# Conditioning sums of gate 0 and layer 1 moved behind layer 0's attention, in pages of their own, half of them on ScalarE and GpSimd

## The chip, the cores and the metric

The kernel runs on one core of one Trainium2 chip. Its time is the device time of one execution in microseconds (us): 2407.33 is the median of three runs (2405.7 to 2408.84). A core has a matrix engine (TensorE, PE in the profile, with its weight loads as PEld), three engines for elementwise work (VectorE or DVE, ScalarE or ACT, GpSimd or POOL) and a queue engine (SyncE or SP) that here issues the large loads. Each works through its own list of instructions in order, and semaphores tie them together. Tiles lie in SBUF, 128 partitions wide; TensorE writes to PSUM, which has 8 banks of 128x512 fp32.

## The reference, cut to what matters

Two transformer blocks on 256 latent tokens and 256 context tokens of width 2048, batch 1. The first block has two layers whose norm and residual are conditioned: a vector `c` (latent) and a vector `c_ctx` (context) each go through a 2048 x 6144 matrix per layer, and the 6144 sums are shift, scale and gate.

```python
for l in range(2):
    last = l == 1
    shift, scale, gate = split(silu(c) @ ada_w[l] + ada_b[l], 3)             # latent
    shift_c, scale_c, gate_c = split(silu(c_ctx) @ ada_w[l] + ada_b[l], 3)   # context
    h  = rmsnorm(x,  norm_g[l]) * (1 + scale)   + shift
    hc = rmsnorm(xc, norm_g[l]) * (1 + scale_c) + shift_c
    # q, k, v, pool, fourier, gate inputs: h @ w_in[l]; the context in layer 1 gives only k and v
    att = attention(q, [kc; k], [vc; v])                # 8 heads of 128, 2 kv heads
    mixed = concat(att, multiscale_pool(up), fourier_mix(uf))
    x = x + gate * ((mixed * silu(g)) @ w_out[l])
    if not last:                                        # the same for the context
        xc = xc + gate_c * outc
# then a second block: w_in (4096 columns), gating, a recurrent scan, w_out, a gated FFN of width 6144
```

`ada_w` is 2 x 2048 x 6144 fp32, 100.7 MB, read once. Layer 1 needs the context's shift and scale but not its gate.

## The kernel before, in words

**Weights.** Every projection is a list of steps. A step asks for one tile of 128x1024 fp32 of a weight (512 KB, `wraw`, a ring of 4), splits it into a rounded part `whi` (a cast on ScalarE, L259) and a remainder `wlo` (a subtraction on VectorE, L260), and multiplies three products per pair (`mm3`, L203 to L205): 24 matmuls of 512 columns, or 24 of 256 where only one half of the tokens is multiplied. `execute` (L111) walks the list: it issues the loads of coming steps on SP in the order of the list (`_issue`, L101), at least 3 ahead, and splits up to 3 weights ahead, with high priority.

**Conditioning.** Layer 0's shift and scale are multiplied on TensorE in the startup, from pages of 128x512 (`apage`, in ring B). All others are summed on VectorE: `ada_span` (L306) covers 512 columns; it loads 8 tiles of two 128x512 blocks into the same `wraw` ring as the weights, and for each of the 16 blocks does one multiply-add by a per-partition column of silu(c) for the latent (accumulator in SBUF, ring E of 2) and, if `nm` is 2, one for the context (accumulator in the PSUM bank `ada`): L322 for the first block, L324 for the others. ScalarE then copies the accumulators to S tiles (L329), and `ada_sum` adds over the partitions with ones on TensorE (L341), transposes (L348) and adds the bias (L355).

**Order.** After the startup, layer 0's list `main` runs: the last quarter of the k, v, q, Fourier and pool projections (9 steps), 32 attention tasks queued, the constants of block 2 queued, pool channels (4 steps), gate groups 2, 3, 0, 1 (8 steps each; all tasks are flushed ahead of group 0, which needs attention's output), and the output projection `w_out`, three groups over both token halves and one group for each half (8 steps each). 14 spans (four of layer 0's gate, eight of layer 1's shift and scale, two of layer 1's gate for the latent alone) make 112 steps, dealt out evenly over the list from its start to 12 steps ahead of its end. The last two spans lie in layer 1's list, from its entry 20 at 0.6 a step.

**Tasks.** The tails (q and k norms, attention heads, pool, Fourier, `ada_sum`) are generators in a queue; `tick` starts up to one per two slots of 1.25 us of TensorE work, four at a time. A planner orders each engine's instructions by priority, which follows the order of the list, and by what it expects to be ready.

**Rings.** B has 12 tiles of 128x512: in the attention of layer 0 they are kT (2), v (2) and qT (8). S (9 tiles) serves short-lived results. Layer 1 uses B for k, q and pool tiles too.

Of the kernel before, what the change touches and what calls it, by code (L numbers as in the profile page):

```python
# [8 lines left out]
F32 = mybir.dt.float32  # L9
F32R = mybir.dt.float32r  # L10
AF = mybir.ActivationFunctionType
ALU = mybir.AluOpType
# [20 lines left out]
class Kern:  # L33
# [22 lines left out]
    def S(self, name, dt=F32, shape=(P, 512)):  # L56
        return self.pg.tile(list(shape), dt, tag="S", bufs=9, name=name)

# [32 lines left out]
    def _issue(self, kind, src, nk, width):  # L91

        if kind == "page":
            raw = self.B("apage")
        else:
            raw = self.pg.tile([P, 1024], F32, tag="wraw", bufs=4, name="wraw")
        dst = raw[:, :width]
        if nk > 1:
            dst = dst.rearrange("p (k c) -> p k c", k=nk)
            src = src.rearrange("(k p) c -> p k c", p=P)  # L100
        self.nc.sync.dma_start(dst, src)  # L101
        return raw
# [8 lines left out]
    def execute(self, steps, ahead=3):  # L111
# [3 lines left out]
        for reqs, fn in steps:  # L115
            n = len(reqs)
            if not n:
                fn()
                continue
            while len(ready) < min(len(plan), p + n + max(ahead, 2 * n)):  # L120
                ready.append(self._issue(*plan[len(ready)]))
# [183 lines left out]

    def ada_span(self, l, c0, nm):  # L306

        w = self.a["ada_w"]
        acc = []

        def step(k0, wt):
            nc = self.nc
            if k0 == 0:
                acc.append(self.E("acc0"))
                if nm == 2:
                    acc.append(self.bank("ada", "acc1"))
            for k in (k0, k0 + 1):
                x = wt[:, (k - k0) * 512:(k - k0 + 1) * 512]
                for m in range(nm):
                    cm = self.silu_c[:, m * 16 + k:m * 16 + k + 1]  # L320
                    if k == 0:
                        nc.vector.tensor_scalar(acc[m], x, cm, None, ALU.mult)  # L322
                    else:
                        nc.vector.scalar_tensor_tensor(acc[m], x, cm, acc[m], ALU.mult, ALU.add)  # L324
            if k0 == KT - 2:
                sums = []
                for m in range(nm):
                    sums.append(self.S("ada_acc"))
                    nc.scalar.copy(sums[m], acc[m])  # L329
                self.defer(self.ada_sum, l, c0, sums)  # L330
        return [([("raw", w[l, k * P:(k + 2) * P, c0:c0 + 512], 2, 1024)],
                 partial(step, k)) for k in range(0, KT, 2)]

# [179 lines left out]
    def bcast_cols(self, col, nt):  # L513
        nc = self.nc
        r = self.misc("rbc")
        for t in range(nt):
            b = self.small("bcw", (P, P))
            if t % 2:
# [156 lines left out]
    def attention(self, g, t, h):  # L675
# [13 lines left out]
        nc.vector.reciprocal(rc, sm)  # L689
        nc.vector.tensor_scalar(p[:, :nk], p[:, :nk], rc, None, ALU.mult)  # L690
        yield 3
# [81 lines left out]
    def layer0(self):  # L773
# [13 lines left out]
        fm = lambda c0, n, evac, **kw: self.proj_fm(w_in, c0, n, ks, hi, lo, NT, evac, **kw)  # L787
        pool = lambda b: (lambda t, ps: self.pool_branch(b + t, ps, NT))
        p01 = fm(1536, 256, pool(0), tags=["misc", "misc"])

# [7 lines left out]
        def part(i):  # L798
            ks = list(range(4 * i, 4 * i + 4))
            st = self.proj_tm(w_in, 1024, 512, ks, hi, lo, 4, lambda t, h, ps: self.part_kv(i, t, ps))  # L800
            for g in range(2):
                st += self.proj_tm(w_in, g * 512, 512, ks, hi, lo, 4, lambda t, h, ps, g=g: self.part_q(i, g, t, ps))
            return st + self.proj_fm(w_in, 2048, 512, ks, hi, lo, NT, partial(self.part_fourier, i)) + [p01[i]]
        parts = [part(i) for i in range(4)]
# [12 lines left out]
        for l, first, last in ((0, 4096, 6144), (1, 0, 4096)):  # L817
            for c0 in range(first, last, 512):
                ada += self.ada_span(l, c0, 2)
        for c0 in range(4096, 5120, 512):  # L820
            ada += self.ada_span(1, c0, 1)
        later = lambda fn, *args: ([], partial(self.defer, fn, *args))
        flush = [([], self.flush)]
        main = [later(self.mix_consts, 0)] + parts[3]
        main += [later(self.attention, g, t, h) for g in range(2) for t in range(4) for h in range(4)]
        main.append(([], self.setup_late))
# [8 lines left out]
        for g in (2, 3, 0, 1):  # L835
            if g == 0:
                main += flush
            elif g == 2:
                main.append(([], lambda: self.until(lambda: self.npf == 8)))
# [36 lines left out]
        for m in (1, 0):  # L876
# [3 lines left out]
            main.append(later(self.h_layer1, m))  # L880
        n_proj = sum(1 for st in main if st[0]) - 12
        out, acc, done = [], 0.0, 0
        for st in main:
            out.append(st)
# [44 lines left out]
    def layer1(self):  # L929
# [35 lines left out]
        ada = []  # L965
        for c0 in range(5120, 6144, 512):
            ada += self.ada_span(1, c0, 1)
        main, ada = self.mix_in(main, ada, first=20, per=0.6)
        steps += main + ada
# [59 lines left out]
    def block2_consts(self):  # L1029
# [3 lines left out]
        lam = self.col("lru_lambda", 0, 8)  # L1033
        T = lambda n: self.one("spl_" + n, [P, 8])
        u, z, z2, s, m = T("u"), T("z"), T("z2"), T("s"), T("m")
        nc.scalar.activation(u, lam, AF.Abs)
# [398 lines left out]
```

## Time and profile before

| | |
|---|---|
| median of three runs | 2407.33 us |
| the profiled execution | 2400.92 us |
| its span, first to last instruction | 2398.9 us |
| PE busy | 2284.9 us (95%) |
| DVE busy | 1628.3 us (68%) |
| ACT busy | 1008.9 us (42%) |
| POOL busy | 208.7 us (9%) |
| conditioning sums on DVE (L324) | 302.5 us, 420 instructions |
| PE's granted clock, mean | 0.981 |

Times are microseconds unless marked ns. A busy PE is not a PE at its peak: matmuls are pipelined and their ends are modelled, so a matmul that waits for its weights can look long. The clock is the mean of TensorE's two levels, 1.2 and 2.4 GHz, as a share of the higher. A row of a group of instructions gives the line, the engine, the operation, what it writes and reads with shapes, the count, busy time and mean, then the engine's idle time just before them and what ended most of it. A row of waits names who waited for whom. An fp32 matmul that is not in the rounded form leaves two records.

### The profile page before, as it was taken

The page shows a single profiled execution, that of the slowest core. Times are in us where ns is not written, and L with a number is a line of the kernel's source. Part 1 is how long each engine was busy: PE and PEld are TensorE (multiplying, and loading weights), DVE is VectorE, ACT ScalarE, POOL GpSimd, SP SyncE. Part 2 cuts the span into 40 slices and gives each one's busy share as a digit, 9 for nine tenths or more (in the row PEclk, how much of TensorE's full clock was granted, in tenths as well). Part 3 has the DMA queues.
Part 4 walks back from the last instruction along what each step waited for, and adds up shares of the span by engine and source line. Part 5 has one row for each costly group of instructions (what it writes and reads, how often), then busy time and mean ns, then how long its engine had stood idle before and what let it go on. Part 6 is the DMA issues. An engine that isn't in the chain of part 4 may idle for free. (4 is left out here: it accounts for less than half of the span.)

```text
span 2398.9 us, 37437 instructions
## 1 busy us (share of the span) xinstructions
PE 2284.9 (95%) x14672; PEld 1991.8 (83%) x14672; DVE 1628.3 (68%) x2603; ACT 1008.9 (42%) x1507; POOL 208.7 (9%) x262
## 2 busy tenths in 40 slices
PE   7999789999798999999999999999999999999998
PEld 3777567877576887889998799999999999988886
DVE  3345987889888786755577966667667666664444
ACT  3321323422322364434454744445445545543433
POOL 1000221010101111010032211110000000000100
PEclk9999889999999999999999999999999999999999
DMA  9866442456766755755554455556666656665554
GB/s 316 277 231 188 135 145 82 136 161 202 233 214 190 256 173 176 221 157 159 182 178 158 141 187 167 193 183 185 185 185 183 184 183 183 215 210 187 186 190 151
DMA packets 202721, 447.89 MB, mean 187 GB/s; under 512 B 15848, under 2 KB 60288, under 8 KB 202544
## 3 DMA queue, kind: packets, MB, share of 16 engines
q1 hardware_dynamic: 193088, 428.93, 57.3%
q0 software_dynamic: 3888, 11.18, 1.4%
q10 hardware_dynamic: 5568, 5.40, 0.7%
q8 instruction: 115, 1.88, 0.3%
q14 instruction: 62, 0.51, 0.1%
HBM read 437.05 MB, written 8.39 MB: 186 GB/s over the span
## 5 line engine op out<-in xcount | busy, mean ns | idle before, releaser
L260 DVE TENSOR_TENSOR wlo<-wraw,whi 128x1024 fp32r<-128x1024 f32 x608 | 749.0, 1236 | 532.8 <-ACT whi L259 529.7
L259 ACT CAST whi<-wraw 128x1024 fp32r<-128x1024 f32 x608 | 635.9, 1049 | 980.8 <-PE acc L204 448.3
L203 PE MATMUL acc<-phi,whi 128*128 128x256 f32 (+1 forms) x1600 | 483.7, 302 | 17.6 <-ACT whi L259 16.4
L205 PE MATMUL acc<-phi,wlo 128*128 128x256 f32 (+1 forms) x1600 | 474.7, 299 | 4.9 <-DVE wlo L260 4.7
L204 PE MATMUL acc<-plo,whi 128*128 128x256 f32 (+1 forms) x1600 | 478.7, 299 | 0.0
L203 PE MATMUL acc<-h3t,whi 128*128 128x256 f32 x1536 | 434.3, 283 | 1.3 <-DVE xT L1257 1.3
L205 PE MATMUL acc<-h3t,wlo 128*128 128x256 f32 x1536 | 433.9, 283 | 0.0
L204 PE MATMUL acc<-h3t,whi 128*128 128x256 f32 x1536 | 433.9, 283 | 0.0
L203 PEld LDWEIGHTS acc<-phi,whi 128*128 128x128 f32 x1600 | 306.2, 191 | 35.2 <-ACT whi L259 21.0
L205 PEld LDWEIGHTS acc<-phi,wlo 128*128 128x128 f32 x1600 | 305.7, 191 | 18.1 <-DVE wlo L260 8.3
L324 DVE SCALAR_TENSOR_TENSOR acc<-wraw,silu_c,acc 128x512 f32<-128x512 f32 x420 | 302.5, 760 | 17.3 <-DMA wraw<-in_ada_w_dram 16.3
L204 PEld LDWEIGHTS acc<-plo,whi 128*128 128x128 f32 x1600 | 306.2, 191 | 9.5 <-issue 0.9
L203 PEld LDWEIGHTS acc<-h3t,whi 128*128 128x128 f32 x1536 | 293.3, 191 | 1.7 <-DVE xT L1257 1.7
L205 PEld LDWEIGHTS acc<-h3t,wlo 128*128 128x128 f32 x1536 | 293.4, 191 | 0.2
L204 PEld LDWEIGHTS acc<-h3t,whi 128*128 128x128 f32 x1536 | 293.4, 191 | 0.0
L203 PE MATMUL acc<-hhi,whi 128*128 128x512 f32 x384 | 167.2, 435 | 10.5 <-ACT whi L259 10.5
L204 PE MATMUL acc<-hlo,whi 128*128 128x512 f32 x384 | 154.7, 403 | 0.0
L204 PE MATMUL acc<-wlo,act 128*128 128x512 f32 x384 | 151.7, 395 | 0.0
L203 PE MATMUL acc<-whi,act 128*128 128x512 f32 x384 | 151.7, 395 | 0.0
L205 PE MATMUL acc<-whi,act 128*128 128x512 f32 x384 | 151.7, 395 | 0.0
L205 PE MATMUL acc<-hhi,wlo 128*128 128x512 f32 x384 | 148.7, 401 | 0.8 <-DVE wlo L260 0.8
L203 PEld LDWEIGHTS acc<-hhi,whi 128*128 128x128 f32 x384 | 73.7, 192 | 36.8 <-ACT whi L259 16.8
(354 smaller groups left out, 2828.1 us busy)
## 6 DMA issues: line engine op xcount, KB each, us to landing
wraw<-in_w_in_dram SPq DMA_DIRECT2D x216, 512.0 KB, 4.2
wraw<-in_ffn_w_up_dram SPq DMA_DIRECT2D x192, 512.0 KB, 3.6
wraw<-in_ada_w_dram SPq DMA_DIRECT2D x128, 512.0 KB, 4.2
wraw<-in_w_out_dram SPq DMA_DIRECT2D x104, 512.0 KB, 4.6
wraw<-in_ffn_w_down_dram SPq DMA_DIRECT2D x96, 512.0 KB, 4.6
apage<-in_ada_w_dram SPq DMA_DIRECT2D x128, 256.0 KB, 5.6
xd<-xT SPq DMA_DIRECT2D x16, 256.0 KB, 3.0
xT<-xd POOLq DMA_DIRECT2D x16, 256.0 KB, 4.6
```

What stands on the lines that cost most here:

```text
L203: mm(out, lhi, rhi, start=start, stop=False)
L204: mm(out, lhi, rlo, start=False, stop=False)
L205: mm(out, llo, rhi, start=False, stop=stop)
L259: self.nc.scalar.copy(hi, src)
L260: self.nc.vector.tensor_tensor(lo, src, f(hi), ALU.subtract)
L324: nc.vector.scalar_tensor_tensor(acc[m], x, cm, acc[m], ALU.mult, ALU.add)
```

## The change

The list of spans is now 12 of two vectors each in layer 0 (four of layer 0's gate, eight of layer 1's shift and scale), dealt out from the end of gate group 2 (`first`) to 10 steps ahead of the end of `main`; layer 1's own four gate spans, for the latent alone, all lie in layer 1's list, from its entry 18 at 1.6 a step. A span's loads are 16 pages of 128x512 (256 KB) from ring B, one step each. The latent's accumulator moves to the PSUM bank and the context's to an E tile. In every span but each fourth (`pool`), the context's half is done by a scaling in place on ScalarE, after VectorE has read the page, and an add on GpSimd into the E tile. Loads now run ahead until two weights beyond the present step are asked for. Weights have 5 tiles, S has 8; the small tiles of the block 2 constants and of the broadcasts move into S. Attention's tasks are queued after each group of q rather than after all parts, and the division by the softmax sum goes from VectorE to ScalarE.

```diff
...
@@ -93,7 +93,7 @@
         if kind == "page":
             raw = self.B("apage")
         else:
-            raw = self.pg.tile([P, 1024], F32, tag="wraw", bufs=4, name="wraw")
+            raw = self.pg.tile([P, 1024], F32, tag="wraw", bufs=5, name="wraw")
         dst = raw[:, :width]
         if nk > 1:
             dst = dst.rearrange("p (k c) -> p k c", k=nk)
@@ -117,7 +117,8 @@
             if not n:
                 fn()
                 continue
-            while len(ready) < min(len(plan), p + n + max(ahead, 2 * n)):
+            while len(ready) < len(plan) and (len(ready) < p + n + max(ahead, 2 * n) or sum(
+                    r[0] == "w" for r in plan[p + n:len(ready)]) < 2):
                 ready.append(self._issue(*plan[len(ready)]))
             while nsplit < len(ready) and (plan[nsplit][0] != "w" or live < 3):
                 if plan[nsplit][0] == "w":
@@ -303,33 +304,34 @@
         ins = nc.vector.scalar_tensor_tensor(self.gs[l][:, t0:t0 + nb, :], ad[:, s, :], 1.0, gain, ALU.add, ALU.mult)
         self.fin = getattr(ins, "ins", ins).name
 
-    def ada_span(self, l, c0, nm):
+    def ada_span(self, l, c0, nm, pool=False):
 
         w = self.a["ada_w"]
         acc = []
 
-        def step(k0, wt):
+        def step(k, x):
             nc = self.nc
-            if k0 == 0:
-                acc.append(self.E("acc0"))
+            if k == 0:
+                acc.append(self.bank("ada", "acc0") if nm == 2 else self.E("acc0"))
                 if nm == 2:
-                    acc.append(self.bank("ada", "acc1"))
-            for k in (k0, k0 + 1):
-                x = wt[:, (k - k0) * 512:(k - k0 + 1) * 512]
-                for m in range(nm):
-                    cm = self.silu_c[:, m * 16 + k:m * 16 + k + 1]
-                    if k == 0:
-                        nc.vector.tensor_scalar(acc[m], x, cm, None, ALU.mult)
-                    else:
-                        nc.vector.scalar_tensor_tensor(acc[m], x, cm, acc[m], ALU.mult, ALU.add)
-            if k0 == KT - 2:
+                    acc.append(self.E("acc1"))
+            for m in range(nm):
+                cm = self.silu_c[:, m * 16 + k:m * 16 + k + 1]
+                if m and pool:
+                    nc.scalar.activation(x if k else acc[m], x, AF.Copy, scale=cm)
+                    if k:
+                        nc.gpsimd.tensor_tensor(acc[m], acc[m], x, ALU.add)
+                elif k == 0:
+                    nc.vector.tensor_scalar(acc[m], x, cm, None, ALU.mult)
+                else:
+                    nc.vector.scalar_tensor_tensor(acc[m], x, cm, acc[m], ALU.mult, ALU.add)
+            if k == KT - 1:
                 sums = []
                 for m in range(nm):
                     sums.append(self.S("ada_acc"))
                     nc.scalar.copy(sums[m], acc[m])
                 self.defer(self.ada_sum, l, c0, sums)
-        return [([("raw", w[l, k * P:(k + 2) * P, c0:c0 + 512], 2, 1024)],
-                 partial(step, k)) for k in range(0, KT, 2)]
+        return [([("page", w[l, k * P:(k + 1) * P, c0:c0 + 512], 1, 512)], partial(step, k)) for k in range(KT)]
 
     def ada_sum(self, l, c0, sums):
         nc = self.nc
...
@@ -687,7 +689,7 @@
         nc.scalar.activation(p[:, :nk], sc[:, :nk], AF.Exp, bias=mx, accum_out=sm)
         rc = self.small("rc", (P, 1))
         nc.vector.reciprocal(rc, sm)
-        nc.vector.tensor_scalar(p[:, :nk], p[:, :nk], rc, None, ALU.mult)
+        nc.scalar.activation(p[:, :nk], p[:, :nk], AF.Copy, scale=rc)
         yield 3
         tp = self.misc("pTp")
         for c in range(nk // P):
...
@@ -800,6 +803,8 @@
             st = self.proj_tm(w_in, 1024, 512, ks, hi, lo, 4, lambda t, h, ps: self.part_kv(i, t, ps))
             for g in range(2):
                 st += self.proj_tm(w_in, g * 512, 512, ks, hi, lo, 4, lambda t, h, ps, g=g: self.part_q(i, g, t, ps))
+                if i == 3:
+                    st += [later(self.attention, g, t, h) for t in range(4) for h in range(4)]
             return st + self.proj_fm(w_in, 2048, 512, ks, hi, lo, NT, partial(self.part_fourier, i)) + [p01[i]]
         parts = [part(i) for i in range(4)]
         steps = ada_chunk(0, 256)
@@ -816,13 +821,9 @@
         ada = []
         for l, first, last in ((0, 4096, 6144), (1, 0, 4096)):
             for c0 in range(first, last, 512):
-                ada += self.ada_span(l, c0, 2)
-        for c0 in range(4096, 5120, 512):
-            ada += self.ada_span(1, c0, 1)
-        later = lambda fn, *args: ([], partial(self.defer, fn, *args))
+                ada += self.ada_span(l, c0, 2, pool=len(ada) // KT % 4 != 3)
         flush = [([], self.flush)]
         main = [later(self.mix_consts, 0)] + parts[3]
-        main += [later(self.attention, g, t, h) for g in range(2) for t in range(4) for h in range(4)]
         main.append(([], self.setup_late))
         main += fm(2048 - 256, 256, pool(2))
         order = list(range(8, 16)) + list(range(8))
@@ -835,6 +836,8 @@
         for g in (2, 3, 0, 1):
             if g == 0:
                 main += flush
+            elif g == 3:
+                first = len(main)
             elif g == 2:
                 main.append(([], lambda: self.until(lambda: self.npf == 8)))
             gate = fm(2560 + g * 512, 512, lambda t, ps, g=g: self.gate(g * 4 + t, ps, NT))
@@ -878,9 +881,9 @@
             main += self.proj_fm(w_out, 1536, 512, order, lambda k, s=s: self.pr[k][0][:, s],
                                  lambda k, s=s: self.pr[k][1][:, s], NX, partial(evac_half, m))
             main.append(later(self.h_layer1, m))
-        n_proj = sum(1 for st in main if st[0]) - 12
-        out, acc, done = [], 0.0, 0
-        for st in main:
+        n_proj = sum(1 for st in main[first:] if st[0]) - 10
+        out, acc, done = main[:first], 0.0, 0
+        for st in main[first:]:
             out.append(st)
             if st[0]:
                 acc += len(ada) / n_proj
@@ -963,9 +966,9 @@
                 main.append(([], self.flush))
             main += self.proj_fm(w_in, 2560 + g * 1024, 1024, ks, hi, lo, NX, partial(evac_g, g))
         ada = []
-        for c0 in range(5120, 6144, 512):
+        for c0 in range(4096, 6144, 512):
             ada += self.ada_span(1, c0, 1)
-        main, ada = self.mix_in(main, ada, first=20, per=0.6)
+        main, ada = self.mix_in(main, ada, first=18, per=1.6)
         steps += main + ada
         order = list(range(8, 16)) + list(range(8))
 
...
```

## Rows read from the trace of the kernel before

**Rows 1.** Busy us (xcount) of PE, PEld, DVE, ACT, POOL by stretch; clock, DMA, GB/s.

```profile
233.00:469.00 236.00, 208.05 (x950) 161.57 (x949) 201.10 (x397) 75.97 (x153) 36.17 (x56) 0.93 0.42 128
469.00:872.00 403.00, 371.21 (x1822) 292.87 (x1821) 340.89 (x565) 127.14 (x195) 43.49 (x52) 0.97 0.65 204
872.00:1060.00 188.00, 175.49 (x1017) 146.02 (x1015) 135.32 (x246) 90.52 (x157) 19.87 (x32) 0.98 0.61 185
1640.00:1660.00 20.00, 20.00 (x171) 20.00 (x170) 8.74 (x8) 7.30 (x8) 0.00 (x0) 1.00 0.62 184
2200.00:2220.00 20.00, 20.00 (x88) 16.05 (x86) 8.57 (x7) 7.74 (x8) 0.00 (x0) 1.00 0.60 188
```

**Rows 2.** Groups of TensorE's instructions, 233 to 469 us: busy us, mean ns, idle before.

```profile
L700 PE MATMUL pv<-pT,v 128*128 128x128 f32 x142 | 19.3, 276 | 0.0
...
L682 PE MATMUL sc<-kT,qT 128*128 128x512 f32 x32 | 16.1, 593 | 0.0
...
L752 PE MATMUL fz<-ab,mix 128*128 128x256 f32 x32 | 9.7, 447 | 3.0 <-DVE mix L618 3.0
```

**Rows 3.** Timeline of TensorE about 402 us: start us, us from first to last end.

```profile
401.83 0.59 PE L682 MATMUL sc<-kT,qT 128*128 128x256 f32 x2
402.27 1.16 PE L700 MATMUL pv<-pT,v 128*128 128x128 f32 x8
403.27 1.04 PE L694 MATMUL pTp<-ident,p 128*128 128x128 f32 x8
404.06 0.48 PE L204 MATMUL acc<-hlo,whi 128*128 128x512 f32 x1
```

**Rows 4.** Groups of TensorE's instructions, 469 to 872 us.

```profile
L203 PE MATMUL acc<-phi,whi 128*128 128x512 f32 x192 | 80.7, 421 | 16.1 <-ACT whi L259 15.9
...
L203 PE MATMUL acc<-phi,whi 128*128 128x256 f32 x128 | 37.3, 291 | 0.5 <-ACT whi L259 0.2 <-DVE xT L855 0.2
```

**Rows 5.** Groups of TensorE's instructions, 872 to 1060 us.

```profile
L203 PE MATMUL acc<-whi,phi 128*128 128x512 f32 x115 | 47.9, 416 | 0.0
...
L203 PE MATMUL acc<-phi,whi 128*128 128x256 f32 x137 | 40.8, 298 | 0.3 <-ACT whi L259 0.3
```

**Rows 6.** Groups of VectorE's instructions, 233 to 469 us.

```profile
L324 DVE SCALAR_TENSOR_TENSOR acc<-wraw,silu_c,acc 128x512 f32<-128x512 f32 x127 | 91.9, 763 | 0.8 <-DMA wraw<-in_ada_w_dram 0.6
```

**Rows 7.** Groups of VectorE's instructions, 469 to 872 us.

```profile
L324 DVE SCALAR_TENSOR_TENSOR acc<-wraw,silu_c,acc 128x512 f32<-128x512 f32 x264 | 188.8, 760 | 6.8 <-DMA wraw<-in_ada_w_dram 6.0
...
L260 DVE TENSOR_TENSOR wlo<-wraw,whi 128x1024 fp32r<-128x1024 f32 x67 | 83.4, 1245 | 39.7 <-ACT whi L259 39.3
```

**Rows 8.** Waits of ScalarE, 469 to 872 us: us in total, times, longest.

```profile
ACT whi L259 <- DMA wraw<-in_w_out_dram: 102.4, 26, 9.7
...
ACT ada_acc L329 <- DVE acc L324: 23.6, 8, 4.7
```

**Rows 9.** Waits of TensorE, 469 to 872 us.

```profile
PE acc L203 <- ACT whi L259: 23.2, 16, 4.9
```

**Rows 10.** The line that issues weight and conditioning loads, 469 to 872 us: ns min/median/max.

```profile
L101 SPq DMA_DIRECT2D wraw<-in_ada_w_dram x76: 367/368/368, 475.3 to 816.2; - x76
...
DMA to landing us min/median/max: 3.5/4.5/6.7
```

**Rows 11.** The line of the conditioning sums, whole span: ns min/median/max.

```profile
L324 DVE SCALAR_TENSOR_TENSOR acc<-wraw,silu_c,acc x420: 731/748/1666, 236.9 to 1038.5; 128x512 f32<-128x512 f32 x140
```

**Rows 12.** The line of layer 0's residual, whole span.

```profile
L855 DVE SCALAR_TENSOR_TENSOR xT<-acc,ad,xT x32: 469/477/484, 693.0 to 871.9; 128x256 f32<-128x256 f32 x32
```

**Rows 13.** Groups of GpSimd's instructions, 469 to 872 us.

```profile
L905 POOL TENSOR_TENSOR sqa<-sqa,sqt 128x512 f32<-128x512 f32 x11 | 17.9, 1627 | 136.8 <-ACT sqt L904 136.6
```

**Rows 14.** The line of the sums of squares, whole span: ns min/median/max.

```profile
L905 POOL TENSOR_TENSOR sqa<-sqa,sqt x19: 721/1394/2131, 697.6 to 874.2; 128x512 f32<-128x512 f32 x11, 128x256 f32<-128x256 f32 x8
```

**Rows 15.** Groups of ScalarE's instructions, 469 to 872 us.

```profile
L904 ACT ACTIVATE sqt<-xT 128x512 f32<-128x512 f32 x11 | 7.0, 634 | 5.3 <-DVE xT L855 5.2
```

**Rows 16.** Busy time by stretch, in the startup.

```profile
40.00:60.00 20.00, 17.04 (x92) 8.92 (x87) 6.71 (x16) 5.81 (x9) 2.61 (x4) 0.91 1.08 351
```

More of the change, by code (lines that the diff above doesn't have):

```diff
@@ L56, in S @@
     def S(self, name, dt=F32, shape=(P, 512)):
-        return self.pg.tile(list(shape), dt, tag="S", bufs=9, name=name)
+        return self.pg.tile(list(shape), dt, tag="S", bufs=8, name=name)
     def half(self, name, i):
@@ L516, in bcast_cols @@
         for t in range(nt):
-            b = self.small("bcw", (P, P))
+            b = self.S("bcw", shape=(P, P))
             if t % 2:
@@ L788, in layer0 @@
         pool = lambda b: (lambda t, ps: self.pool_branch(b + t, ps, NT))
+        later = lambda fn, *args: ([], partial(self.defer, fn, *args))
         p01 = fm(1536, 256, pool(0), tags=["misc", "misc"])
@@ L1033, in block2_consts @@
         lam = self.col("lru_lambda", 0, 8)
-        T = lambda n: self.one("spl_" + n, [P, 8])
-        u, z, z2, s, m = T("u"), T("z"), T("z2"), T("s"), T("m")
+        spl = self.S("spl", shape=(P, 5, 8))
+        u, z, z2, s, m = (spl[:, i] for i in range(5))
         nc.scalar.activation(u, lam, AF.Abs)
```

## The prediction

> **What bounds the kernel now.** The page's busy shares put TensorE at 95%, but a waiting matmul counts as busy there, so I read counts by stretch first, then each engine's groups, then the waits. Three stretches matter: stage A, 233 to 469 us (from the end of the startup to the end of gate group 2), stage B, 469 to 872 us (gate groups 3, 0, 1 and layer 0's output projection), and stage L, 872 to 1060 us (layer 1 up to its attention) [rows 1]. From about 1200 us on the diff changes only spare buffers, so I expect nothing there. The last two lines there give TensorE's pace when nothing holds it: 88 matmuls of 512 columns in 20 us are 0.227 us each, 171 of 256 columns 0.117 us.
>
> From these and the counts I work out what TensorE needs. Stage A issues 21 weight steps of 24 matmuls: 504 x 0.227 = 114 us. The rest is plain fp32, and the timeline shows its pace: two records of a 256-column score start 0.44 us ahead of the next instruction, so 0.22 each (and 0.44 for 512), 8 records of pv take 1.00 us, 8 transposes 0.79 us [rows 3]. With the counts of [rows 2]: 32 score records x 0.44 = 14, 16 of half width 3.5, 142 pv x 0.125 = 18, 71 transposes (one for each two records of pv) 7, Fourier 32 + 64 records x 0.22 = 21, pool, q, k and constants by the same prices 10. Together 187 us of 236: 49 are lost. Stage B by the same count: three lines, two projections, 192 each, and 41 of layer 1's first step, 1193 x 0.227 = 271, 383 x 0.117 = 45 [rows 4], about 25 for the rest: 341 of 403, 62 lost. Stage L: 345 x 0.227 + 410 x 0.117 [rows 5] + about 41 for attention = 167 of 188, 21 lost.
>
> What loses it: VectorE is busy 201 of 236 and 341 of 403 us [rows 1], and the conditioning sums are the largest group on it, 92 us in A [rows 6] and 189 in B [rows 7]. They also share the 4-slot ring of weight tiles. In B ScalarE's cast stands 102 us in 26 waits for a weight of w_out that has not landed [rows 8], although a transfer lands 4.5 us after its issue [rows 10]: it was issued late, behind conditioning tiles that VectorE had not yet released. TensorE then waits for the cast, 23 us of plain waits [rows 9].
>
> **The change part by part.** The profiled execution took 2400.92 us, 2398.9 of span and 2.0 around it; the median of the runs is 2407.33, so 6.4 above. I sum against the first and add 6.4.
>
> *Stage A.* The first four spans go: 4 x 32 = 128 VectorE operations, 92 us in the trace [rows 6], and their transfers. VectorE's load falls from 201 to about 109 of 236 us, less still because the softmax normalisation moves to ScalarE, which is busy only 76 of 236. What is late next is the chain of norm, GpSimd power and transpose per q tile, and the 8 pool and Fourier results that gate 2 waits for; queueing group 0's attention earlier puts TensorE work beside it. Bounds: to TensorE's 187 us (-49) or nothing (0), if those chains and not VectorE hold it. The nearest row is stage L, the same work with 30 of these operations instead of 128 and 11% lost: 187 / 0.89 = 210. A little of the sums' cost is still in that 11%, so I take 207: **-29**.
>
> *Stage B.* All 12 spans now lie in 54 weight steps, 3.56 pages of 256 KB a step. Of these 3 spans cost VectorE 32 operations and 9 only 16: 240 against the 280 that the trace has here (416 by the code, 136 of them before 469 us), at 0.75 us -30 [rows 7], so 311 us. New are 9 x 16 = 144 scalings on ScalarE; the nearest row is a 512-column Square in SBUF, 0.634 us [rows 15], so at least 91 us, and with a scale pointer I take 104; 127 + 104 of 403 leaves it room. New on GpSimd are 9 x 15 = 135 adds. The same add of the same shape took 1.627 us on the mean of 11 [rows 13] and up to 2.131 [rows 14]: 220 us with the 43 already there, 263.
>
> What GpSimd's adds cost VectorE: a sum operation next to them took up to 1.666 instead of 0.748 us [rows 11]. The diff puts the accumulator of VectorE's half into PSUM; the residual operation, which reads PSUM and runs beside GpSimd's adds, never took over 0.484 [rows 12]. So I charge only the operations with two SBUF inputs, some 80 (the splits of weights, 1.245 us each [rows 7], of products, and the gates): from 0 to 0.92 each, I take 0.4, 32 us. VectorE comes to 343, TensorE with three more sums to 344. The Trainium skill (GPSIMD Engine Reference, § 1 Specifications) says that GpSimd's SBUF interfaces are shared with VectorE and that the conflict is with operations in a two-port mode or with two SBUF inputs. The two rows fit it; were PSUM operands hit as well, 144 more operations at 0.4 would add 58 us.
>
> The rings part: 12 pages for the sums, 5 tiles for weights. Weights then no longer wait for VectorE's sums, but all transfers stay in one queue on SP, in order: a page that waits for GpSimd's add holds the weights behind it. SP issues some 116 more transfers at 0.368 us [rows 10], 40 us of an idle queue. GpSimd's own queue has the reloads of x behind the adds; they are used 8 weight steps later, which covers several adds. Bytes: 82 MB now (204 GB/s x 403), 76 conditioning tiles (40 MB) out [rows 10], 50 in: 92 MB in 380 us are 243 GB/s, against 351 reached in the startup [rows 16]. Bounds of B: 344 (-59), if TensorE alone is left, to 432 (+29), if GpSimd binds at 2.131 us (135 x 2.131 + 43 + 101 for three spans of VectorE alone). VectorE and TensorE are now equal, and two equal engines don't mesh fully: at the 90% that stage L shows, 344 / 0.9 = 382. I take 380: **-23**.
>
> *Stage L and after.* Two spans more, 32 operations of 0.748 us, so 24 us of VectorE, which is busy 135 of 188, and 64 pages instead of 16 tiles; the pages share their 12 buffers with layer 1's q, k and v. Bounds 0 to +24; VectorE has 53 us free, but the tail of a span sits where attention ends: **+6**.
>
> S tiles 9 to 8 and the small tiles moved into them: nothing, TensorE runs full in the long later stretch its last two lines [rows 1]; without that cover a wait for an S tile costs about one 512-column operation, 0.75 us.
>
> Sum: -29 - 23 + 6 = **-46**, so 2355 on the profiled execution and **2361** on the median.
>
> **The rivals.**
> *GpSimd becomes the bound of stage B.* For: its load there goes from 43 to 263 us, and in the pool spans VectorE's splits slow its adds. Against: at 1.627 us it still has 117 us free. It binds from (380 - 101 - 43) / 135 = 1.75 us per add; at 1.95, between mean and longest, B takes 407: -29 + 4 + 6 = -19, **2388**. The skill's page speaks for this rival (GPSIMD Engine Reference, § 4.1 Engine selection: an elementwise add belongs to VectorE, GpSimd is about 2x slower); 1.627 against 0.748 us agrees with the price, but says nothing of which engine is full.
>
> *The hand-over through ScalarE makes it slower.* Each of 144 pages goes VectorE, ScalarE in place, GpSimd, and ScalarE, which works in order, also casts each weight. If it stands before a scaling until VectorE has read the page, the cast behind it comes late and TensorE waits. For: ScalarE already stood 23.6 us in 8 waits, 3 us each, for the sums' last operation [rows 8]. Against: casts have a high priority in the written order, and three split weights lie ahead. A wait can be as long as one sum operation, 0.75 us; at 0.5 us a page, 72 us fall on the path: **2433**. It decides from 46 / 144 = 0.32 us a page.
>
> *The change frees VectorE, but stage A does not move,* because the q chain and the wait for 8 results hold it: -23 + 6 = -17, **2390**. For: TensorE's clock is granted at 0.93 there [rows 1], so it idles in lumps.
>
> **How the numbers follow.** Forecast 0.55, GpSimd 0.15, hand-over 0.20, stage A unmoved 0.10. The forecast's own range is 2320 to 2392 (A -15 to -49, B -10 to -50, L 0 to +12, not all ends together). All ends together give 2299 and 2460. The range for 8 in 10 is 2322 to 2428: it takes in the GpSimd and stage A cases and the milder half of the hand-over. About 0.2% (5 us) is what a measurement can tell from no change. Faster: 0.55 + 0.11 of GpSimd's + 0.08 of stage A's = 0.74; within: 0.03 + 0.02 = 0.05; slower: the hand-over 0.20 and 0.01 = 0.21.
>
> **What would show it.** Right: stage A ends near 440 us instead of 469 with VectorE near half busy; stage B then lasts about 380 us, the cast's waits for weights fall well below 102 us, GpSimd is busy about 260 us in it at some 1.6 us per add, and sums in PSUM keep 0.75 us. Wrong: adds at 1.75 us or more with SP waiting for GpSimd; ScalarE waiting for VectorE ahead of scalings, with TensorE waiting for the cast longer than 23 us; stage A still at 236; or a loss in stage L above 15 us, with VectorE waiting there for pages.

## The result and the profile after

The changed kernel takes 2367.82 us (median of four, 2362.87 to 2368.59), the kernel before 2406.51 (2403.93 to 2408.84): a ratio of 0.9835, 95% interval 0.9818 to 0.9852, so 38.7 us faster. 2361 was forecast, in the range 2322 to 2428. The profiled execution took 2368.4 us, 32.5 less than that of before (2400.92). The profiled execution of before lies 5.6 us below its median, that of after 0.6 above.

First the page: the span, and each engine's busy time.

```profile
span 2366.6 us, 38158 instructions
...
PE 2269.3 (96%) x14672; PEld 1992.3 (84%) x14672; DVE 1561.9 (66%) x2411; ACT 1126.6 (48%) x1699; POOL 407.1 (17%) x397
```

Then the busy time by stretch, in the columns of [rows 1]. The ends are the same events as there: the end of gate group 2 (469, now 446), the last evacuation of layer 0's residual (872, now 847) and, 10 us behind layer 1's first pool tile, 1060, now 1022.

```profile
233.00:446.00 213.00, 203.20 (x974) 159.85 (x975) 117.73 (x263) 99.67 (x199) 56.22 (x71) 0.98 0.28 88
446.00:847.00 401.00, 371.06 (x1823) 299.03 (x1822) 342.15 (x467) 212.97 (x322) 218.77 (x172) 0.96 0.68 216
847.00:1022.00 175.00, 163.96 (x972) 136.59 (x970) 144.90 (x257) 96.46 (x170) 22.36 (x32) 0.98 0.72 232
```

Against [rows 1], stage A went from 236 to 213 us (-23), B from 403 to 401 (-2), L from 188 to 175 (-13), and what follows from 1338.9 to 1344.6 (+6). Read so, A gained most of what was forecast and B almost nothing. But the stretches no longer hold the same work. The counts of TensorE's groups show what moved. In before's stage B, with its 14 records of a layer 1 projection:

```profile
L700 PE MATMUL pv<-pT,v 128*128 128x128 f32 x53 | 7.7, 274 | 0.0
L203 PE MATMUL acc<-whi,phi 128*128 128x512 f32 x14 | 5.5, 395 | 0.0
L682 PE MATMUL sc<-kT,qT 128*128 128x256 f32 x16 | 4.9, 384 | 0.0
L694 PE MATMUL pTp<-ident,p 128*128 128x128 f32 x24 | 4.3, 274 | 0.3 <-DVE p L690 0.3
```

The same groups after the change, and the conditioning sums' own matmuls (`ada_ps`), before which TensorE now stands idle 12.2 us for ScalarE's copy:

```profile
L204 PE MATMUL acc<-whi,phi 128*128 128x512 f32 x31 | 12.2, 395 | 0.0
L343 PE MATMUL ada_ps<-ada_acc,ones 128*32 128x256 f32 x96 | 10.3, 401 | 12.2 <-ACT ada_acc L332 12.2
L702 PE MATMUL pv<-pT,v 128*128 128x128 f32 x28 | 4.2, 274 | 0.0
L684 PE MATMUL sc<-kT,qT 128*128 128x256 f32 x10 | 3.0, 378 | 0.0
L696 PE MATMUL pTp<-ident,p 128*128 128x128 f32 x12 | 2.3, 273 | 0.0
```

Three forms of the layer 1 projection went from 13 or 14 to 31 records each, 52 matmuls at 0.227 us, 12 us of work pulled from L into B. 25 pv records, 12 transposes and 6 half scores, by the prediction's prices 6 us, left B, and most of them went to A, while A lost some 2.5 us of the sums' matmuls. With equal work A gained some 26 us, B 5 to 8 and L 2 to 3. These are estimates from the counts; the sum over A, B and L, -38, needs none.

Now VectorE's, GpSimd's and ScalarE's groups of stage B (446 to 847 us).

```profile
L327 DVE SCALAR_TENSOR_TENSOR acc<-apage,silu_c,acc 128x512 f32<-128x512 f32 x210 | 155.8, 767 | 2.7
L261 DVE TENSOR_TENSOR wlo<-wraw,whi 128x1024 fp32r<-128x1024 f32 x72 | 107.6, 1494 | 19.3 <-ACT whi L260 18.4
L261 DVE TENSOR_TENSOR plo<-mix,phi 128x512 fp32r<-128x512 f32 x16 | 15.7, 978 | 0.2
...
L323 POOL TENSOR_TENSOR acc<-acc,apage 128x512 f32<-128x512 f32 x120 | 179.6, 1497 | 103.7 <-ACT apage L321 91.8 <-DMA wraw<-in_w_out_dram 5.0
...
L321 ACT ACTIVATE apage<-apage,silu_c 128x512 f32<-128x512 f32 x120 | 83.4, 719 | 47.9 <-DVE acc L327 39.7 <-issue 5.0 <-ACT apage L321 1.4
```

And the waits there (us in total, times, longest). `ada_acc` is ScalarE's copy of a span's accumulator, `ada_ps` the matmul that adds it up, `ada_sb` ScalarE's copy of that sum, `ada_t` its transpose:

```profile
ACT whi L260 <- PE acc L205: 42.9, 24, 4.8
ACT apage L321 <- DVE acc L327: 39.7, 29, 6.1
ACT ada_acc L332 <- POOL acc L323: 24.5, 6, 7.5
...
PE ada_ps L343 <- ACT ada_acc L332: 12.2, 3, 7.5
PE ada_t L350 <- ACT ada_sb L346: 11.0, 3, 6.2
...
ACT whi L260 <- DMA wraw<-in_w_out_dram: 1.0, 1, 1.0
```

The cast's wait for weights of w_out fell from 102.4 us in 26 waits [rows 8] to 1.0 in one. TensorE's 23.2 us behind the cast [rows 9] are gone, and 12.2 + 11.0 us have come in their place (2.5 us at the transpose were there before): it now stands at the conditioning sums' own matmul and transpose. The two have different causes. The longest stop at the matmul is shown by timelines (start, duration; in brackets the idle time before it and what ended it). First GpSimd, up to its last add of a span:

```profile
707.23 4.03 POOL L908 TENSOR_TENSOR sqa<-sqa,sqt 128x512 f32<-128x512 f32 x3
...
712.45 0.75 POOL L452 DMA_DIRECT2D rope<-in_k_cos_dram  x1
...
719.14 1.27 POOL L323 TENSOR_TENSOR acc<-acc,apage 128x512 f32<-128x512 f32 x1
```

ScalarE's copy, which waits for it at the head of ScalarE's queue, and TensorE's sum, which waits for the copy:

```profile
720.44 0.62 ACT L332 COPY ada_acc<-acc 128x512 f32<-128x512 f32 x1 [7.51 <-POOL acc L323]
...
721.11 1.07 PE L343 MATMUL ada_ps<-ada_acc,ones 128*32 128x256 f32 x4 [7.50 <-ACT ada_acc L332]
```

The add ends at 720.41, the copy starts at 720.44, the matmul at 721.11. VectorE's half was ready by 712.4, when ScalarE copied it; the slower half sets the end of the span. GpSimd was late because other work stood in its queue between the last adds: sums of squares (L908) and the loads of layer 1's tables (L452, `rope`). VectorE waited for that table too, and only then split the next weight:

```profile
716.10 0.62 DVE L466 TENSOR_TENSOR rope_q<-rope,gb_q 128x256 f32<-128x256 f32 x1 [5.39 <-DMA rope<-in_k_cos_dram]
...
720.96 1.21 DVE L261 TENSOR_TENSOR wlo<-wraw,whi 128x1024 fp32r<-128x1024 f32 x1
```

TensorE needs that split for the next step's products, so an earlier copy alone would have left a stop about there; e1 below has one of 4.7 us.

The longest stop at the transpose has nothing to do with GpSimd. Both halves were summed at 535.06, but ahead of the copy of the sum ScalarE had a scaling of another span in its queue, and that stood for its page:

```profile
543.88 0.72 ACT L321 ACTIVATE acc<-apage,silu_c 128x512 f32<-128x512 f32 x1 [8.97 <-DMA apage<-in_ada_w_dram]
...
544.92 0.69 PE L350 MATMUL ada_t<-ident,ada_sb 128*128 128x128 f32 x2 [6.22 <-ACT ada_sb L346]
```

The third, 4.43 us at 755, came behind six scalings and a cast that ScalarE did ahead of the same copy, having itself stood 6.29 us for GpSimd just before.

### The profile page after: what moved, and what is told of

It reads as the page before. It is cut to its first block, busy times and chain, and to the rows that moved or that the text cites. A ratio compares the mean times of both kernels' runs of the same rounds, so it can differ in the third digit from the quotient of the medians.

```text
span 2366.6 us, 38158 instructions
## 1 busy us (share of the span) xinstructions
PE 2269.3 (96%) x14672; PEld 1992.3 (84%) x14672; DVE 1561.9 (66%) x2411; ACT 1126.6 (48%) x1699; POOL 407.1 (17%) x397
## 4 chain that ended last, share of the span: by engine, by line
PE 66%; DVE 6%; issue 5%; POOL 3%; ACT 2%; DMA 2%; POOLq 0%; ACTq 0%; SPq 0%; DVEq 0%
PE acc L204 21%; PE acc L205 21%; PE acc L206 21%; DVE wlo L261 1%; POOL acc L323 1%; DVE acc L327 1%; DMA apage<-in_ada_w_dram 1%; PE pv L702 1%; ACT whi L260 1%; PE sc L684 1%; PE pTp L696 0%; POOL qrs L495 0%; DMA wraw<-in_w_in_dram 0%; DVE lr L1174 0%; DMA gw_n<-in_gm_ws_dram 0%
## 5 line engine op out<-in xcount | busy, mean ns | idle before, releaser
L261 DVE TENSOR_TENSOR wlo<-wraw,whi 128x1024 fp32r<-128x1024 f32 x608 | 767.6, 1265 | 550.4 <-ACT whi L260 538.9
L323 POOL TENSOR_TENSOR acc<-acc,apage 128x512 f32<-128x512 f32 x135 | 199.7, 1479 | 128.7 <-ACT apage L321 115.7
L327 DVE SCALAR_TENSOR_TENSOR acc<-apage,silu_c,acc 128x512 f32<-128x512 f32 x285 | 211.5, 761 | 10.8 <-DMA apage<-in_ada_w_dram 7.4
```

The source lines that it names most:

```text
L261: self.nc.vector.tensor_tensor(lo, src, f(hi), ALU.subtract)
L323: nc.gpsimd.tensor_tensor(acc[m], acc[m], x, ALU.add)
```

## The experiments

Ratios are to the kernel before, run on the same chip. Stretches are cut at the same evacuations as above, L at layer 1's first pool tile: before A 236, B 403, L 178 us; after 213, 401, 165 (the expectations have 565 for B and L together, here it is 566). Each diff is against the changed kernel.

**e1: the copy of GpSimd's half later.** ScalarE's copy of GpSimd's accumulator is issued six turns later, inside the deferred sum.

```diff
 for m in range(nm):
+    if m and pool:
+        late = acc[m]
+        continue
     sums.append(self.S("ada_acc"))
...
+        yield 6
+        sums.append(self.S("ada_acc"))
+        nc.scalar.copy(sums[1], late)
```

> In the nine spans that share the work, the copy of GpSimd's accumulator on ScalarE moves from the end of the span into the later task, six slots (about 7.5 us of TensorE work) on; nothing else changes. Theory W (the gain of stage B, 401 us after the change where 380 was forecast, is held by a new wait: ScalarE stands 24.5 us for GpSimd's last add ahead of that copy, and TensorE stands 23 us at the sums' matmul and transpose): both waits fall below 8 us, stage B becomes 380 to 390 us, the kernel 2348 to 2360. Theory V (VectorE's 342 us of work in stage B, with splits at 1.49 us, is the bound): the waits only move to the cast or the split, stage B stays within 5 us of 401, the kernel within 6 us of 2368.

Measured: 2361.97 us, ratio 0.9822 (0.9802 to 0.9842). Stage B 393 us instead of 401: both lie between the two theories. Its waits there (446 to 840 us):

```profile
ACT ada_acc L345 <- POOL acc L323: 19.4, 4, 7.6
...
PE ada_t L358 <- ACT ada_sb L354: 11.2, 4, 6.2
...
PE ab_ps L493 <- DMA fourier_w<-in_fourier_w_dram: 4.7, 1, 4.7
```

TensorE's 12.2 us at the sum's matmul are gone and those at the transpose stayed. The stop of 7.50 us shrank to the 4.7 of the last line, at the same point of the program: TensorE now waits for another of layer 1's tables, loaded from GpSimd's queue behind its adds. So a later copy took about a third of the new loss; the 6 us in the median lie at the edge of what these runs tell apart.

**e2: all sums on VectorE**, in the new place and the new pages.

```diff
-ada += self.ada_span(l, c0, 2, pool=len(ada) // KT % 4 != 3)
+ada += self.ada_span(l, c0, 2)
```

> All twelve spans are summed by VectorE alone; pages, places and rings stay as changed. Theory V and the prediction: VectorE gets 135 operations of 0.75 us back and loses about 25 us of slowed splits, 342 + 101 - 25 = 418 us in stage B, so the stage lasts 430 to 445 us and the kernel 2395 to 2412. Rival (the sharing gives back by its waits what it saves): stage B within 8 us of 401, the kernel within 8 us of 2368.

Measured: 2386.21, ratio 0.9917 (0.9898 to 0.9935); B and L together 584 us instead of 566. VectorE is busy 366.59 of 396 us, with no adds of the sums beside it (444 to 840 us):

```profile
L327 DVE SCALAR_TENSOR_TENSOR acc<-apage,silu_c,acc 128x512 f32<-128x512 f32 x337 | 234.6, 754 | 2.9 <-DMA apage<-in_ada_w_dram 2.8
L261 DVE TENSOR_TENSOR wlo<-wraw,whi 128x1024 fp32r<-128x1024 f32 x65 | 79.9, 1229 | 17.4 <-ACT whi L260 17.3
```

So sharing the sums out is worth 18 us, and the rest of the change, place and rings above all, some 20. The time lies between the two expectations. The loss fell in L (189), not in B as expected: spans that VectorE could not end in B ran on beside layer 1. TensorE still stood at the sums' matmul, with no half on GpSimd, so that wait does not come from the sharing alone:

```profile
PE ada_ps L343 <- ACT ada_acc L332: 14.4, 3, 8.7
```

**e3: the softmax division back on VectorE.**

```diff
-nc.scalar.activation(p[:, :nk], p[:, :nk], AF.Copy, scale=rc)
+nc.vector.tensor_scalar(p[:, :nk], p[:, :nk], rc, None, ALU.mult)
```

> The division by the softmax sum goes back to VectorE in both layers. Theory 1 (it matters little: VectorE has room in both attention stretches): stages A and L within 4 us of 213 and 175, the kernel within 5 us of 2368. Theory 2 (the unexpected gain of stage L, 175 instead of 188 us, comes from this): stage L 183 to 190 us, the kernel 2376 to 2382.

Measured: 2370.72, ratio 0.9854 (0.9836 to 0.9873), A 215 instead of 213. This part of the change matters little.

**e4: attention queued behind all parts, as before.**

```diff
-if i == 3:
-    st += [later(self.attention, g, t, h) for t in range(4) for h in range(4)]
...
+main += [later(self.attention, g, t, h) for g in range(2) for t in range(4) for h in range(4)]
```

> Attention's 32 tasks of layer 0 are queued after all parts again, as in the kernel before; the rest stays as changed. Theory 1 (stage A gained its 23 us because the sums left VectorE): stage A within 6 us of 213, the kernel 2364 to 2376. Theory 2 (the earlier order did it): stage A 228 to 236 us, the kernel 2382 to 2392.

Measured: 2360.41, ratio 0.9816 (0.9797 to 0.9834); A 203, B 407, L 166. Both lie outside either theory, on the side of theory 1: A's gain does not need the earlier attention. What remains is that the sums left the stage. They took their work off VectorE and their tiles out of the weights' ring, where ScalarE's cast had stood 57.2 us for weights (233 to 469 us) and now stands 6.2 (233 to 446 us); no run parts the two:

```profile
ACT whi L259 <- DMA wraw<-in_w_in_dram: 57.2, 15, 9.8
...
ACT whi L260 <- DMA wraw<-in_w_in_dram: 6.2, 1, 6.2
```

A is 10 us shorter and B 6 longer, partly the attention that moved back; that the order costs time at all is indicated (7 us, intervals that overlap), not shown.

**e5: sums spread up to the half groups only.** The same pages over 47 weight steps instead of 54, 4.09 a step.

```diff
-n_proj = sum(1 for st in main[first:] if st[0]) - 10
+n_proj = sum(1 for st in main[first:] if st[0]) - 17
```

> The twelve spans are dealt over 47 weight steps instead of 54, so that they end ahead of the output projection's two half groups, whose steps take half the TensorE time. Theory H (pages are dealt by steps, so the last span meets steps of 2.8 us; the first half group takes 42 us instead of 28): that group returns to 28 to 32 us, the denser pages cost 3 to 6 us before it, the kernel 2356 to 2364. Rival (the work is only shifted): the groups before lengthen by what the half groups save, the kernel within 4 us of 2368.

Measured: 2384.35, ratio 0.9918 (0.9905 to 0.9931), B 413. Both expectations missed it: denser pages cost 17 us. From the end of gate group 1 to that of w_out group 2 it took 189 us against 163, while the first half group fell from 42 to 24. TensorE's wait for the copies doubled:

```profile
PE ada_ps L343 <- ACT ada_acc L332: 28.4, 11, 7.4
PE acc L204 <- DVE xT L858: 9.6, 2, 7.0
```

**e6: sums all on VectorE, in two-block tiles of the weights' own ring** (five tiles), at the new place. In layer 1's list the spans go at 0.8 a step, since a step now holds two blocks.

```diff
-return [([("page", w[l, k * P:(k + 1) * P, c0:c0 + 512], 1, 512)], partial(step, k)) for k in range(KT)]
+return [([("raw", w[l, k * P:(k + 2) * P, c0:c0 + 512], 2, 1024)], partial(step, k)) for k in range(0, KT, 2)]
...
+ada += self.ada_span(l, c0, 2)
```

> As the run with all sums on VectorE, but the sums' tiles are again pairs of blocks in the weights' ring, now 5 tiles, in place of pages of their own. Theory R (the separate ring is what lets weights arrive early): the cast's waits for weights come back to over 60 us in stage B, stages B and L together last 592 to 610 us instead of 584, the kernel 2393 to 2412. Rival (only the place of the sums counts): the kernel within 5 us of that run's 2386.

Measured: 2415.68, ratio 1.0048 (1.0031 to 1.0064), slower than before. From 446 to 860 us:

```profile
ACT whi L260 <- DMA wraw<-in_w_out_dram: 141.0, 30, 8.6
...
ACT whi L260 <- DMA wraw<-in_w_in_dram: 48.5, 12, 6.7
...
PE acc L204 <- ACT whi L260: 33.1, 17, 5.3
```

Both waits of [rows 8] and [rows 9] are back, and larger. Against e2, which has the same sums on the same engine and its own pages, the shared ring costs 29.5 us (ratios 1.0048 and 0.9917). e2 has the 12 pages on top of the five tiles, so a ring of one's own and more room come together here; no run gave the shared ring that room. Moving the sums into the old kind of ring lost.

**e7: VectorE's accumulator in SBUF instead of PSUM.**

```diff
-acc.append(self.bank("ada", "acc0") if nm == 2 else self.E("acc0"))
+acc.append(self.S("acc0") if nm == 2 else self.E("acc0"))
```

> VectorE's accumulator of the shared spans lies in an SBUF tile of ring S instead of the PSUM bank; nothing else changes. Theory P (VectorE's operations with two SBUF inputs and GpSimd's adds slow each other, those with a PSUM input don't): the sums' operation in stage B goes from 0.767 to 0.95 to 1.2 us on the mean, GpSimd's add from 1.50 to over 1.6, the kernel 2380 to 2400. Rival (what slows them is something else): both within 5% of their values, the kernel within 6 us of 2368.

Measured: 2435.02, ratio 1.0128 (1.0111 to 1.0145), 67 us above the changed kernel. Its groups, 446 to 900 us:

```profile
L327 DVE SCALAR_TENSOR_TENSOR acc<-apage,silu_c,acc 128x512 f32<-128x512 f32 x225 | 250.9, 1138 | 2.9
L261 DVE TENSOR_TENSOR wlo<-wraw,whi 128x1024 fp32r<-128x1024 f32 x65 | 104.7, 1612 | 17.2 <-ACT whi L260 17.1
...
L323 POOL TENSOR_TENSOR acc<-acc,apage 128x512 f32<-128x512 f32 x135 | 222.3, 1647 | 181.7 <-ACT apage L321 174.3
```

And the longest of ScalarE's waits there:

```profile
ACT apage L321 <- DVE acc L327: 109.3, 73, 5.2
```

The sum operation costs 1.138 us on the mean when its accumulator lies in SBUF, 0.767 in the changed kernel and 0.754 in e2 with no such adds. That mean mixes two kinds. Of the same line, the shortest, median and longest operation in ns are, here (446 to 900 us) and in e12 (446 to 850 us), where every span is shared and every such accumulator lies in PSUM:

```profile
L327 DVE SCALAR_TENSOR_TENSOR acc<-apage,silu_c,acc x225: 735/752/1897, 453.5 to 879.6; 128x512 f32<-128x512 f32 x113
...
L327 DVE SCALAR_TENSOR_TENSOR acc<-apage,silu_c,acc x165: 739/756/757, 471.7 to 796.0; 128x512 f32<-128x512 f32 x165
```

By the times in the traces, 112 of e7's 225 met no GpSimd add and took 754 ns on the mean; 104 lay beside one for most of their time and took 1583. In e12 145 of 165 lay beside one and none took over 757. VectorE is busy 421.35 of 454 us, and TensorE waits for VectorE itself:

```profile
PE acc L204 <- DVE th L771: 20.7, 4, 15.5
PE acc L204 <- DVE xT L858: 16.8, 2, 9.1
```

ScalarE's wait ahead of scalings, the sign of the hand-over rival, grew to 109 us, but TensorE has no wait for the cast of a weight in this stretch: by these waits the loss came through VectorE's slower operations, not through the hand-over. The kernel came out worse than expected. The edit moves the accumulator in all twelve spans of layer 0's list, not in the shared ones alone, and it also takes a tile of ring S for as long as a span lasts; no run has an accumulator in SBUF without that.

**e8, e9: sums of edits.** e9 is e1 and e4 together, e8 these and e5.

```diff
+        nc.scalar.copy(sums[1], late)
...
+main += [later(self.attention, g, t, h) for g in range(2) for t in range(4) for h in range(4)]
```

> Three edits together: GpSimd's accumulator copied six slots later, attention queued after all parts, the spans ended ahead of the half groups. If each takes its own wait away (-6 and -7 us measured, -6 expected): 2345 to 2354. If they free the same slack: 2357 to 2363.

> The late copy of GpSimd's accumulator and the old order of attention together, the spans dealt over 54 steps as changed. If each takes a wait of its own away (6 and 7 us measured alone): 2352 to 2358. If they free the same slack: 2359 to 2364.

Measured: e8 2374.69, ratio 0.9879 (0.9865 to 0.9894), which neither expectation has; it holds e5's edit, which lost alone. e9 2361.92, ratio 0.9822 (0.9807 to 0.9837), the same as either edit alone, as the second expectation has it. The gains are not additive: TensorE's wait at the transpose stayed in e9 as in e1.

**e10: e9 with another span in each four kept whole on VectorE.**

```diff
-ada += self.ada_span(l, c0, 2, pool=len(ada) // KT % 4 != 3)
+ada += self.ada_span(l, c0, 2, pool=len(ada) // KT % 4 != 2)
```

> As the run with these two edits, with VectorE's full spans at the third, seventh and eleventh place instead of the fourth, eighth and twelfth, so that the last span, which meets the half groups, is shared. If the half groups are held by VectorE's 32 operations in the last span: 4 to 10 us less, 2344 to 2352. If they run at TensorE's pace already (326 matmuls in 42 us): within 4 us of that run.

Measured: 2367.49, ratio 0.9846 (0.9831 to 0.9861), 5.6 worse than e9; neither expectation has that. Taking VectorE's full span away from the end did not help. One wait of TensorE for GpSimd's sums of squares grew from 1.9 to 7.0 us, which has the size, but no run shows that it is the cause.

**e11: layer 0's sums of squares from GpSimd to VectorE.**

```diff
-self.sum_sq(self.sqa[:, s], xT[:, s], k == 0)
+self.sum_sq(self.sqa[:, s], xT[:, s], k == 0, nc.vector)
```

> The adds of squares of layer 0's residual go from GpSimd to VectorE, about 24 us of GpSimd's 219 in stage B; the rest stays as changed. Theory G (GpSimd binds in the third group of the output projection, where it is busy 55 of 64 us): that group falls from 64 to 55 to 59 us, the kernel 2359 to 2364. Theory V (VectorE binds there): the group stays or grows, the kernel 2368 to 2376.

Measured: 2375.68, ratio 0.9878 (0.9861 to 0.9894), 8 us worse. VectorE has 352.58 of 414 us busy, these adds among them:

```profile
L908 DVE TENSOR_TENSOR sqa<-sqa,sqt 128x512 f32<-128x512 f32 x11 | 10.7, 973 | 0.4 <-ACT sqt L907 0.4
```

w_out group 2 (the third), where GpSimd was busy 55 of 64 us after the change, still took 63, as theory V has it. So GpSimd's total is not the bound even there.

**e12: every span shared.**

```diff
-ada += self.ada_span(l, c0, 2, pool=len(ada) // KT % 4 != 3)
+ada += self.ada_span(l, c0, 2, pool=True)
```

> All twelve spans are shared, not nine. VectorE loses 48 operations (36 us) in stage B, GpSimd gets 45 adds (68 us) more, 287 of 401. Theory V (VectorE binds in the full spans): stages B and L together fall by 5 to 15 us from 565, the kernel 2354 to 2363. Theory G (GpSimd and the hand-over bind): they grow by 5 to 25 us, the kernel 2373 to 2393.

Measured: 2367.0, ratio 0.9842 (0.9827 to 0.9857), no change, between the two theories, though VectorE fell to 315.46 us of 404 and GpSimd rose to 295.91.

```profile
PE ada_t L350 <- ACT ada_sb L346: 20.6, 5, 7.4
```

VectorE's total isn't the bound any more either: 27 us off it gave nothing, while TensorE's waits at the sums' tail rose from 23.2 to 29.8 us (9.2 of them at the matmul).

No version beats the changed kernel clearly: e4, e9 and e1 are 6 to 7 us below it, with intervals that overlap its own.

## Why the prediction was right, step by step

**Stage A, -29: right in kind, a little too large.** -23 by the cut, some 26 gained with equal work. VectorE fell from 201 to 118 us (about 109 was forecast), and TensorE's granted clock rose from 0.93 to 0.98. The rival in which A doesn't move is out. Neither the earlier attention (e4: 203 without it) nor ScalarE's division (e3: 215 without it) made the gain; whether VectorE's time or the ring did is not shown.

**Stage B, -23: the term that was mis-sized.** -2 by the cut, 5 to 8 gained with equal work. Its parts came out close. VectorE: 342 us, 343 forecast. Scaling: 0.719 us, 0.72 forecast. GpSimd: 1.497 us an add, 1.627 forecast, and 219 us where 263 were forecast, 15 of the 135 adds having run ahead in A. Slower operations with two SBUF inputs: against e2 the weight splits took 0.265 us more each (72, 19 us) and those of products 978 instead of 685 ns (16, 5 us), so 24 us with 32 forecast. Sums in PSUM kept 0.767. The Trainium skill's rule (GPSIMD Engine Reference, § 1 Specifications: the conflict with VectorE is with two-port modes or two SBUF inputs) agrees with e7 and e12: beside GpSimd's adds the sum took 1583 ns with both inputs in SBUF, at most 757 with one in PSUM.

What failed is the last line of that step, the 90% of meshing taken from stage L: 344 / 401 is 86%, and 350 / 401 is 87% with the 6 us of matmuls that the stage took on. The forecast left 36 us of loss and named no wait for it; the runs showed 51. TensorE stood idle 29.9 us (401 - 371.06), 23.2 of them at the sums' own matmul and transpose; that this equals the 23.2 that went is chance. 12.2 us came at the end of a span, where GpSimd's half was late behind its other work and ScalarE's copy stood in order for it; 11.0 at the transpose, nearly all of it behind scalings that ScalarE had ahead, in the longest stop one that waited for a page. e1 takes the first part away, 4.7 us come back in its place, and B falls by 7. What is left of the 51 us lies in matmuls that run slowly; some of it is the clock after each stop (last section).

**Stage L, +6: wrong in sign.** -13 by the cut, 2 to 3 gained with equal work. The 24 us of VectorE's new operations were covered; the loss expected from a span's tail at the end of attention didn't come. By the cut B and L together gave -15, close to the -17 forecast, and that is luck: the one term was too hopeful and the other too dark, and some 6 us of attention had moved to A. With equal work it is 7 to 11.

**The later stretch, 0:** +6 in this profile. From layer 1's first pool tile to the end it is 1349 us before, 1355 after and 1351 to 1356 in the experiments. The 1349 come from one execution, 5.6 us below its kernel's median, and these 6 us are as much as parts the 32.5 us of the profiles from the 38.7 of the medians. Whether the change lost a few us here stays open.

**Rivals.** GpSimd as the bound by its total is out (e11, e12, adds at 1.5 us); by its lateness at the end of a span it decided part of B, which the forecast didn't separate. The Trainium skill's advice (GPSIMD Engine Reference, § 4.1 Engine selection: elementwise adds to VectorE) agrees in price, 1497 against 767 ns, and goes against the runs as a choice of place: with all sums on VectorE, then busy 367 of 396 us, e2 is 18 us slower. The hand-over through ScalarE costs 39.7 us of ScalarE's waits, 0.33 us a page; that reaches the 0.32 from which it was to decide, but TensorE's wait for the cast vanished, so these waits did not reach TensorE: the casts ran far enough ahead to stand 42.9 us themselves until TensorE had used up earlier weights. In e7 they grew to 109 us and still made TensorE wait for no cast of a weight, so no run carries this rival to the time.

**Where the gain came from.** The runs split B and L (581 us before): with the sums moved, all on VectorE and the shared ring they take 615 (e6), with their own pages 584 (e2), with half of most spans on ScalarE and GpSimd 566 (after). In the shared ring the move loses although A gains its 23 us; with pages of their own it pays 20 us, and the sharing adds 18. Sharing the sums while their tiles stay in the weights' ring was not run.

**Open:** the 7 us of the earlier attention, e10's loss, w_out group 2 (58 us before, 64 after; two stops of TensorE there, 7.50 and 4.43 us, tell most of its loss, but e11 didn't shorten it); how much of A's gain is VectorE's and how much the ring's; ring or room in e6.

## What to carry to other kernels

When work leaves a full engine for two slower ones, price the tail as well as the total: the slowest half of the last piece sets when its consumer runs, and an engine that works in order and copies the result stands with all that is queued behind it. Read that engine's own queue before naming the culprit: of the three longest stops here one had GpSimd at its root, one a page that had not landed, one ScalarE's own scalings. Bulk loads that share a ring with the tiles on the critical path take the pace of whoever releases the bulk; a ring of their own, with the room that it brought, was worth 29 us here, more than the two further engines (18). Before reading a gain by stretch, count the instructions in it: the scheduler moves work across any cut.

## What the runs showed of the hardware beyond the forecast

One operand decides how two engines disturb each other: the sum took 754 ns with no GpSimd add beside it, at most 757 beside them with the accumulator in PSUM (e12), and 1583 with it in SBUF (e7). GpSimd suffers too: its adds took 1497 ns on the mean beside PSUM sums and 1647 beside SBUF sums. The weight splits, with two SBUF inputs always, took 1229 ns on the mean in e2, 1494 in the changed kernel and 1612 in e7.

A stop of TensorE costs more than its length. After the stop of 7.50 us the granted clock was the lower level, 0.50 (1.2 GHz), and matmuls of 512 columns started 0.43 us apart (723.13, 723.56); just before it they had started 0.23 apart (712.40, 712.63), and a little later the clock was 1.00 again:

```profile
721.00:725.00 4.00, 3.89 (x11) 2.50 (x12) 3.89 (x6) 2.12 (x5) 0.47 (x1) 0.50 0.68 188
...
733.00:737.00 4.00, 4.00 (x18) 3.20 (x17) 3.89 (x6) 3.19 (x6) 3.84 (x3) 1.00 0.87 287
```

Over whole stretches the granted clock was 0.98 in stage A after the change, where TensorE was busy 203.20 of 213 us, and 0.89 in e7's stage B, where it was busy 374.67 of 454.
